# Four z blocks and five gate blocks named ahead of the query stage, an order edge behind them, and a fifth query and key buffer

## The chip, the core and the metric

The kernel runs on one core of one Trainium2 chip. The metric is the device time of one execution in microseconds; lower is better. A measured value is the median of several runs, and one execution is profiled.

## What is computed

One layer of a hybrid encoder over 1024 tokens of width 1024, all in float32. A shared RMS norm and one wide input projection feed two branches: a Hyena branch (two gated long convolutions) and an attention branch with low-rank queries and keys. The lines that matter here:

```
h = rms_norm(x, g_norm);  proj = h @ w_in
hy_in, z_hy, c_q, c_kv, k_rope, z_attn, gate_hy, gate_attn = split(proj)
... hyena branch: zc from hy_in by two long convolutions, u_hy = (zc * silu(z_hy)) @ w_hy_out
q  = rms_norm(c_q, g_cq) @ w_uq            # 8 heads of 96
kv = rms_norm(c_kv, g_ckv) @ w_ukv         # 64 key columns and 64 value columns a head
q, k = rms_norm per head, rotary on the last 32 columns (the key's come from k_rope)
u_attn = (softmax(q k^T) v * silu(z_attn)) @ w_attn_out
gates = sigmoid([gate_hy, gate_attn] + b_gate)
out = x + (g_hy * u_hy + g_at * u_attn) @ w_out
```

## The kernel before, in words

**Tiling.** Everything is done in blocks of 128 rows or columns. A float32 operand of a product is split into a high and a low part (`split`, L138 on ScalarE and L139 on VectorE; `gsplit`, L142 and L143, the same with a scale), and each product is three matmuls: high by high, low by high, high by low (`mm3`, L119 to L122).

**Projection blocks.** `proj_block` (L567) makes one block of 128 columns of `proj` for all tokens: 48 matmuls of 128x512, in two halves of 24. Each half loads a weight tile `wr` on the SP queue (L559, two buffers) and splits it into `wh` and `wl` (four buffers each). The result lies in two PSUM banks `pm` out of four, so that two blocks can be under way. Three kinds of blocks matter: `fill_c` (query and key latents, `cT`), `fill_z` (four blocks of `z_attn`; a sigmoid on ScalarE at L673, then VectorE, then a store on SP) and `fill_g` (sixteen gate blocks; a sigmoid at L683 and a store that ScalarE issues, L684). Their sigmoids free the banks.

**The stages.** After the norm and the filter spectra, with gate blocks 0 to 7 among them, come the convolutions (`convs`), then `qkv`, then `attention`, then the output products. `qkv` makes queries, keys and values for eight tiles of 128 tokens, in four pairs (`hf` 0 to 3). Its weights pass through `wst` (two buffers: three loads of `w_uq` at L735, then two of `w_ukv`; then the rotary table `rt` at L753 and the raw rotary key `kr` at L764 use the same buffers). Per tile: six query products in `pq` (two banks, 18 matmuls of 128x384, evicted by L795 into `q`), products of keys and values in `pkv` (12 matmuls of 128x512, evicted by L799 and L800 into `k` and `v`). The rotary key is transposed for all tiles at once (`pkr`, L767), and every tile's key norm needs it. Per pair: sums of squares (L803 to L808), a reciprocal root on VectorE (`rsqrt`, L152 to L158), the scaling of the queries (L813), their rotary part (`rot`, L827 to L830), the keys on GpSimd (L818, L819), and stores of `q` and `k` on SP (L822). `q` and `k` have four buffers each, and a buffer is free when its store has landed.

**What comes behind.** `load_pair` (L838) loads the first two heads' queries, keys and values back (`qr`, `kr`, `vr`). `attention` opens PSUM pools in the banks that the projection blocks held, so it starts behind the last block's sigmoid. It begins with transposes (L862) into `pth`, split by L142 into `qh`, `kh`. The weights of the Hyena output (`branch_out`, L981, `wr` with two buffers; split by ScalarE at L138 and by GpSimd at L139) are loaded early too.

**What sets the order.** No order is written by hand. A scheduler at build time gives every engine its instruction list: of what it holds to be ready by its own cost estimates, it takes first what stands earlier in the program. So instructions that stand later can be placed in the gaps of earlier ones. On the chip each engine then runs its list in order. A call of `behind` (used by `mm3` for its first matmul) adds an edge: that instruction is not placed before another one. In the program, `qkv` stands ahead of the four z blocks and of gate blocks 8 to 15.

Of the kernel before, what the change touches and what calls it, by code (L numbers as in the profile page):

```python
# [10 lines left out]
F32 = mybir.dt.float32  # L11
# [8 lines left out]
P = 128  # L20
# [3 lines left out]
H = 8  # L24
# [9 lines left out]
GEARLY = 8  # L34
# [59 lines left out]
class K:  # L94
# [457 lines left out]
    def proj_block(self, c0, m=P):  # L552

        nc, wp = self.nc, self.wp
        ps = [self.pp.tile([P, 512], F32, tag="mm", bufs=MMB, name=self.nm("pm")) for _ in range(2)]
        src = self.a["w_in"][0].rearrange("(d p) c -> p d c", p=P)
        for g in range(2):
            raw = wp.tile([P, 4, P], F32, tag="wr", bufs=2, name=self.nm("wr"))
            nc.sync.dma_start(out=raw[:, :, 0:m], in_=src[:, 4 * g:4 * g + 4, c0:c0 + m])  # L559
            wh = wp.tile([P, 4, P], F32R, tag="wh", bufs=4, name=self.nm("wh"))  # L560
            wl = wp.tile([P, 4, P], F32R, tag="wl", bufs=4, name=self.nm("wl"))
            self.split(raw[:, :, 0:m], wh[:, :, 0:m], wl[:, :, 0:m])
            for i in range(4):
                d = 4 * g + i
                for (w, h, f) in ((wh, self.hh, 0), (wh, self.hl, 1), (wl, self.hh, 2)):
                    for c in range(2):
                        nc.tensor.matmul(ps[c][0:m], lhsT=w[:, i, 0:m], rhs=h[d][:, c * 512:(c + 1) * 512],  # L567
                                         start=(d == 0 and f == 0), stop=(d == 7 and f == 2))
        return ps

# [150 lines left out]
    def qkv(self, kp):  # L721

        nc, a = self.nc, self.a
# [4 lines left out]
        wqh = kp.tile([P, 3, 768], F32R, tag="wqh", name="wqh")  # L728
        wql = kp.tile([P, 3, 768], F32R, tag="wql", name="wql")
        wkh = kp.tile([P, 2, 1024], F32R, tag="wkh", name="wkh")  # L730
        wkl = kp.tile([P, 2, 1024], F32R, tag="wkl", name="wkl")
        def weights(nme, n, w, wh, wl):
            for c in range(n):
                r = kp.tile([P, w], F32, tag="wst", bufs=2, name=self.nm("wst"))
                nc.sync.dma_start(out=r, in_=a[nme][0, c * P:(c + 1) * P])  # L735
                self.split(r, wh[:, c], wl[:, c])

        def latent(hf, i):
# [4 lines left out]
            self.gsplit(r, self.gcq[:, i:i + 1] if i < 3 else self.gckv[:, i - 3:i - 2], h_, l_)  # L743
            return h_, l_

        weights("w_uq", 3, 768, wqh, wql)
        C = {(0, i): latent(0, i) for i in range(3)}
        weights("w_ukv", 2, 1024, wkh, wkl)
# [29 lines left out]
        for hf in range(4):  # L778
# [5 lines left out]
            for j in range(2):  # L784
                tt = 2 * hf + j
                ts = slice(j * P, (j + 1) * P)
                q = kp.tile([P, H, 96], F32, tag="q", bufs=4, name=self.nm("q"))
                k = kp.tile([P, H, 96], F32, tag="k", bufs=4, name=self.nm("k"))
                v = kp.tile([P, H, 64], F32, tag="v", bufs=2, name=self.nm("v"))
                for g in range(2):  # L790
                    hs = slice(4 * g, 4 * g + 4)
                    ps = self.pp.tile([P, 4, 96], F32, tag="cv", bufs=CVB, name=self.nm("pq"))
                    for c in range(3):
                        self.mm3(ps, ch[c][:, ts], cl[c][:, ts], wqh[:, c, g * 384:(g + 1) * 384], wql[:, c, g * 384:(g + 1) * 384], c == 0, c == 2)
                    nc.scalar.activation(out=q[:, hs], in_=ps, func=AF.Copy, scale=rq0[:, tt:tt + 1])  # L795
                    ps = self.pp.tile([P, 4, 2, 64], F32, tag="tp", bufs=2, name=self.nm("pkv"))
                    for c in range(2):
                        self.mm3(ps, ch[3 + c][:, ts], cl[3 + c][:, ts], wkh[:, c, g * 512:(g + 1) * 512], wkl[:, c, g * 512:(g + 1) * 512], c == 0, c == 1)
                    nc.scalar.activation(out=k[:, hs, 0:64], in_=ps[:, :, 0], func=AF.Copy, scale=rk0[:, tt:tt + 1])  # L799
                    nc.scalar.activation(out=v[:, hs], in_=ps[:, :, 1], func=AF.Copy, scale=rk0[:, tt:tt + 1])  # L800
                nc.sync.dma_start(out=self.vd[:, :, tt].rearrange("b p j c -> p b (j c)"), in_=v.rearrange("p (b j) c -> p b (j c)", j=2))
                sq = kp.tile([P, H, 96], F32, tag="sqq", bufs=2, name=self.nm("sqq"))
                nc.scalar.activation(out=sq, in_=q, func=AF.Square)  # L803
                nc.vector.tensor_reduce(out=ssq[:, j, 0], in_=sq, axis=AX.X, op=ALU.add)
                sk = kp.tile([P, H, 64], F32, tag="sqq", bufs=2, name=self.nm("sqk"))
                nc.scalar.activation(out=sk, in_=k[:, :, 0:64], func=AF.Square)
                nc.vector.tensor_reduce(out=ssq[:, j, 1], in_=sk, axis=AX.X, op=ALU.add)
                nc.vector.tensor_scalar(out=ssq[:, j, 1], in0=ssq[:, j, 1], scalar1=ssr[:, tt:tt + 1], scalar2=None, op0=ALU.add)  # L808
                QK.append((tt, q, k))
# [384 lines left out]
def hyena_mla_kernel(ctx, tc, a, out):  # L1194
# [4 lines left out]
    with k.pool("pp", space=PSUM) as k.pp:  # L1199
        with ExitStack() as sr:  # L1200
# [33 lines left out]
            k.rp = srp.enter_context(k.pool("rp"))  # L1234
            k.raw = {}
            k.load_pair(0)
            for b in range(4):
                k.fill_z(b)
            for b in range(GEARLY, 16):
                k.fill_g(b)  # L1240
            k.hyena_tiles(yp)
    with k.pool("gp2", side="right") as g2:
# [50 lines left out]
```

## Time and profile before

| what | us |
|---|---|
| median of 3 runs (1146.56 to 1151.04) | 1148.81 |
| the profiled execution's own time | 1145.55 |
| its span | 1143.8 |
| TensorE busy in the span | 1094.3 (96%) |
| VectorE busy | 893.9 (78%) |
| ScalarE busy | 588.0 (51%) |
| GpSimd busy | 108.3 (9%) |

The mean granted TensorE clock is 0.997 of full speed. The profiled execution is 3.26 us (0.28%) shorter than the median of the runs, and 1.75 us of its time lie outside the span. Engines in the profile: PE is TensorE's matmuls, PEld its weight loads, DVE is VectorE, ACT is ScalarE, POOL is GpSimd, SP is the engine that issues most loads; SPq is its queue. A busy PE says nothing of how well it is used, and shares over the whole span mix stages; the stage between the convolutions and the attention runs from about 618 to 719 us.

### The profile page before, as it was taken

The page shows a single profiled execution, that of the slowest core. Times are in us where ns is not written, and L with a number is a line of the kernel's source. Part 1 is how long each engine was busy: PE and PEld are TensorE (multiplying, and loading weights), DVE is VectorE, ACT ScalarE, POOL GpSimd, SP SyncE. Part 2 cuts the span into 40 slices and gives each one's busy share as a digit, 9 for nine tenths or more (in the row PEclk, how much of TensorE's full clock was granted, in tenths as well). Part 3 has the DMA queues.
Part 4 walks back from the last instruction along what each step waited for, and adds up shares of the span by engine and source line. Part 5 has one row for each costly group of instructions (what it writes and reads, how often), then busy time and mean ns, then how long its engine had stood idle before and what let it go on. Part 6 is the DMA issues. An engine that isn't in the chain of part 4 may idle for free.

```text
span 1143.8 us, 15469 instructions
## 1 busy us (share of the span) xinstructions
PE 1094.3 (96%) x5525; PEld 905.2 (79%) x5525; DVE 893.9 (78%) x1583; ACT 588.0 (51%) x1101; POOL 108.3 (9%) x112
## 2 busy tenths in 40 slices
PE   4899999999999999999999989899999999999998
PEld 3678888888888888878887878687887878777886
DVE  6988798688788985768865795688788888468984
ACT  6745645754435534533433752787877777221420
POOL 0000000000000000000000042202200000114345
PEclk9989999999999999999999999999999999999999
DMA  5446455642234325234236557501302000897064
GB/s 213 134 147 195 154 166 181 202 123 67 88 92 129 112 85 163 84 95 130 84 92 202 154 157 248 184 29 50 117 5 98 1 19 11 268 312 269 29 198 165
DMA packets 119221, 150.27 MB, mean 131 GB/s; under 512 B 8548, under 2 KB 82408, under 8 KB 119144
## 3 DMA queue, kind: packets, MB, share of 16 engines
q1 hardware_dynamic: 107400, 120.45, 34.2%
q10 hardware_dynamic: 11744, 28.84, 6.7%
q8 instruction: 43, 0.70, 0.3%
q14 instruction: 34, 0.28, 0.1%
HBM read 101.81 MB, written 47.45 MB: 131 GB/s over the span
## 4 chain that ended last, share of the span: by engine, by line
PE 71%; DVE 13%; ACT 6%; DMA 5%; issue 2%; POOL 0%; SPq 0%; ACTq 0%; DVEq 0%; POOLq 0%
PE pm L567 31%; PE pu L128 8%; PE pt L907 4%; PE pi L128 4%; PE pmo L121 2%; PE pmo L119 2%; PE pmo L122 2%; PE S L119 2%; PE S L122 2%; ACT pr L893 2%; PE S L121 2%; PE pv L919 2%; PE pv L920 2%; PE po L119 1%; PE po L122 1%
## 5 line engine op out<-in xcount | busy, mean ns | idle before, releaser
L567 PE MATMUL pm<-hh,wh 128*128 128x512 f32 x656 | 208.8, 394 | 1.8 <-DVE hl L143 0.9
L567 PE MATMUL pm<-hl,wh 128*128 128x512 f32 x656 | 209.0, 394 | 0.0
L567 PE MATMUL pm<-hh,wl 128*128 128x512 f32 x656 | 208.5, 393 | 0.1
L138 ACT CAST wh<-wr 128x512 fp32r<-128x512 f32 x98 | 60.2, 621 | 169.2 <-PE pm L567 107.4
L567 PEld LDWEIGHTS pm<-hh,wh 128*128 128x128 f32 x656 | 123.2, 189 | 27.6 <-DVE hl L143 1.1
L567 PEld LDWEIGHTS pm<-hh,wl 128*128 128x128 f32 x656 | 123.3, 188 | 25.8 <-DVE wl L139 0.5
L567 PEld LDWEIGHTS pm<-hl,wh 128*128 128x128 f32 x656 | 123.0, 188 | 25.2
L138 ACT CAST PTh<-pt 128x512 fp32r<-128x512 f32 x128 | 72.8, 587 | 40.8 <-PE pt L907 39.3
L139 DVE TENSOR_TENSOR PTl<-pt,PTh 128x512 fp32r<-128x512 f32 x128 | 83.8, 682 | 10.6 <-ACT PTh L138 10.1
L891 DVE TENSOR_REDUCE mx<-S 128x1 f32<-128x1024 f32 x64 | 77.9, 1217 | 11.5 <-PE S L122 11.3
L907 PE MATMUL pt<-ident,pr 128*128 128x128 f32 x512 | 75.3, 276 | 3.6 <-ACT pr L893 1.4
L139 DVE TENSOR_TENSOR wl<-wr,wh 128x512 fp32r<-128x512 f32 x95 | 66.1, 700 | 15.5 <-ACT wh L138 15.3
L893 ACT ACTIVATE pr<-S,mx 128x1024 f32<-128x1024 f32 x64 | 71.7, 1120 | 5.2 <-DVE mx L891 4.9
L907 PEld LDWEIGHTS pt<-ident,pr 128*128 128x128 f32 x512 | 58.5, 140 | 19.4 <-DVE PTl L139 5.1
L919 PE MATMUL pv<-PTh,vc 128*128 128x256 f32 x256 | 69.1, 298 | 0.4 <-DVE at L930 0.4
L920 PE MATMUL pv<-PTl,vc 128*128 128x256 f32 x256 | 67.9, 293 | 0.0
L473 DVE TENSOR_TENSOR t<-pu,kt 128x512 f32<-128x512 f32 x64 | 41.1, 682 | 31.6 <-PE pu L128 31.0
L138 ACT CAST rh<-res 128x512 fp32r<-128x512 f32 x64 | 39.5, 619 | 41.7 <-PE pu L128 19.9
L119 PE MATMUL S<-kh,qh 96*128 96x512 f32 x128 | 53.0, 414 | 2.6 <-ACT pr L893 2.4
L121 PE MATMUL S<-kh,ql 96*128 96x512 f32 x128 | 52.2, 408 | 0.0
L919 PEld LDWEIGHTS pv<-PTh,vc 128*128 128x128 f32 x256 | 48.5, 190 | 4.6 <-DVE at L930 1.9
L122 PE MATMUL S<-kl,qh 96*128 96x512 f32 x128 | 51.5, 403 | 0.0
(285 smaller groups left out, 2385.5 us busy)
## 6 DMA issues: line engine op xcount, KB each, us to landing
wr<-in_w_in_dram SPq DMA_DIRECT2D x82, 256.0 KB, 3.2
wor<-in_w_out_dram SPq DMA_DIRECT2D x36, 256.0 KB, 4.3
dec<-in_dec_dram SPq DMA_DIRECT2D x16, 512.0 KB, 3.7
gT<-ob ACTq DMA_DIRECT2D x16, 512.0 KB, 3.0
gg<-gT SPq DMA_DIRECT2D x16, 512.0 KB, 4.7
kd<-kt ACTq DMA_DIRECT2D x28, 256.0 KB, 2.1
kt<-kd SPq DMA_DIRECT2D x28, 256.0 KB, 2.7
m<-gg ACTq DMA_DIRECT2D x16, 256.0 KB, 5.1
```

The source lines that it names most:

```text
L119: m = nc.tensor.matmul(out, lhsT=lh, rhs=rh, start=start, stop=False)
L121: nc.tensor.matmul(out, lhsT=ll, rhs=rh, start=False, stop=False)
L122: nc.tensor.matmul(out, lhsT=lh, rhs=rl, start=False, stop=stop)
L128: m = self.nc.tensor.matmul(out, lhsT=x, rhs=y, start=n == 0, stop=n == len(ops) - 1)
L138: self.behind(self.nc.scalar.copy(out=hi, in_=x), after)
L139: (eng or self.nc.vector).tensor_tensor(out=lo, in0=x, in1=hi.bitcast(F32), op=ALU.subtract)
L567: nc.tensor.matmul(ps[c][0:m], lhsT=w[:, i, 0:m], rhs=h[d][:, c * 512:(c + 1) * 512], start=(d == 0 and f == 0), stop=(d == 7 and f == 2))
L891: nc.vector.tensor_reduce(out=mx, in_=ps, axis=AX.X, op=ALU.max, negate=True)
L893: i = nc.scalar.activation(out=pr, in_=ps, func=AF.Exp, bias=mx, accum_out=RS[h // 2][:, qb, h % 2:h % 2 + 1])
L907: nc.tensor.transpose(out=pt[:, i], in_=pr[:, kb * P:(kb + 1) * P], identity=self.ident)
L919: nc.tensor.matmul(pv, lhsT=V[h][:, kb], rhs=hi[:, kb], start=(kb == 0), stop=False)
L920: nc.tensor.matmul(pv, lhsT=V[h][:, kb], rhs=lo[:, kb], start=False, stop=(kb == 7))
```

## The change

The four z blocks and gate blocks 8 to 12 are written inside `qkv`, ahead of its weight loads; gate blocks 13 to 15 stay where they were. The last matmul of block 12 is kept in `lastmm`, and the first query matmul (tile 0, first half of the heads, first slice) gets an edge behind it. The `q` and `k` tiles get five buffers in place of four, which takes 2 x 3072 bytes more in each partition. Arithmetic, loads and stores are the same in number and size.

```diff
@@ proj_block
-                        nc.tensor.matmul(ps[c][0:m], lhsT=w[:, i, 0:m], rhs=h[d][:, c * 512:(c + 1) * 512],
+                        self.lastmm = nc.tensor.matmul(ps[c][0:m], lhsT=w[:, i, 0:m], rhs=h[d][:, c * 512:(c + 1) * 512],
@@ qkv
+        for b in range(4):
+            self.fill_z(b)
+        for b in range(GEARLY, 13):
+            self.fill_g(b)
+        first = self.lastmm
         weights("w_uq", 3, 768, wqh, wql)
@@ qkv, for each tile
-                q = kp.tile([P, H, 96], F32, tag="q", bufs=4, name=self.nm("q"))
-                k = kp.tile([P, H, 96], F32, tag="k", bufs=4, name=self.nm("k"))
+                q = kp.tile([P, H, 96], F32, tag="q", bufs=5, name=self.nm("q"))
+                k = kp.tile([P, H, 96], F32, tag="k", bufs=5, name=self.nm("k"))
...
-                        self.mm3(ps, ch[c][:, ts], cl[c][:, ts], wqh[:, c, g * 384:(g + 1) * 384], wql[:, c, g * 384:(g + 1) * 384], c == 0, c == 2)
+                        self.mm3(ps, ch[c][:, ts], cl[c][:, ts], wqh[:, c, g * 384:(g + 1) * 384], wql[:, c, g * 384:(g + 1) * 384], c == 0, c == 2,
+                                 first if tt == 0 and g == 0 and c == 0 else None)
@@ hyena_mla_kernel
-            for b in range(4):
-                k.fill_z(b)
-            for b in range(GEARLY, 16):
+            for b in range(13, 16):
                 k.fill_g(b)
```

## Rows read from the trace of the kernel before

**Rows 1.** Chain that ended last, 600 to 745 us: start us, us, what.

```profile
618.19 5.74 DMA wst<-in_w_uq_dram
...
637.84 4.37 DMA kr<-cT
...
655.88 2.67 DVE q L813 x2
...
693.56 2.68 DVE q L813 x2
...
700.71 3.98 DMA qd<-q
...
706.16 6.78 DMA wr<-in_w_hy_out_dram
...
716.23 3.97 DMA wr<-in_w_hy_out_dram
```

**Rows 2.** Three stretches: length, then busy us (count) of PE, PEld, DVE, ACT, POOL.

```profile
622.70:642.20 19.50, 16.21 (x81) 13.72 (x79) 13.43 (x22) 13.93 (x26) 0.00 (x0) 1.00 0.88 280
...
655.90:683.50 27.60, 24.66 (x122) 21.47 (x122) 26.74 (x60) 17.37 (x37) 11.92 (x10) 1.00 0.51 153
...
683.50:700.70 17.20, 17.20 (x77) 14.21 (x77) 16.68 (x39) 5.71 (x11) 7.48 (x7) 1.00 0.69 216
```

**Rows 3.** Timeline of PE: start us, us, line, tile; idle before it and releaser in brackets.

```profile
625.25 0.62 PE L119 MATMUL pq<-wqh,ch 128*128 128x384 f32 x2 [2.18 <-ACT ch L142]
...
633.66 0.44 PE L119 MATMUL pq<-wqh,ch 128*128 128x384 f32 x1
...
642.26 0.71 PE L767 MATMUL pkr<-ident,kr 64*128 64x64 f32 x8 [0.98 <-DMA kr<-cT]
...
666.59 0.45 PE L119 MATMUL pq<-wqh,ch 128*128 128x384 f32 x1 [2.03 <-ACT q L795]
...
683.57 0.63 PE L567 MATMUL pm<-hh,wh 128*128 128x512 f32 x2
...
717.14 0.61 PE L567 MATMUL pm<-hh,wl 128*128 128x512 f32 x2
...
719.31 1.08 PE L862 MATMUL pth<-ident,qr 128*96 128x128 f32 x8 [1.55 <-ACT ob L683]
```

**Rows 4.** Timeline of ACT, columns as in the timeline of PE.

```profile
517.07 1.08 ACT L673 ACTIVATE ob<-pm 128x512 f32<-128x512 f32 x2
...
617.97 1.26 ACT L683 ACTIVATE ob<-pm,cols 128x512 f32<-128x512 f32 x2
...
661.77 0.47 ACT L799 ACTIVATE k<-pkv,ry 128x256 f32<-128x256 f32 x1 [2.63 <-DMA kdr<-k]
...
665.95 1.05 ACT L795 ACTIVATE q<-pq,ry 128x384 f32<-128x384 f32 x2 [2.62 <-DMA qd<-q]
...
696.11 1.26 ACT L683 ACTIVATE ob<-pm,cols 128x512 f32<-128x512 f32 x2
...
712.96 1.37 ACT L138 CAST wh<-wr 128x512 fp32r<-128x512 f32 x2 [15.59 <-DMA wr<-in_w_hy_out_dram]
...
714.24 1.26 ACT L683 ACTIVATE ob<-pm,cols 128x512 f32<-128x512 f32 x2
...
718.05 0.62 ACT L138 CAST wh<-wr 128x512 fp32r<-128x512 f32 x1 [2.55 <-DMA wr<-in_w_hy_out_dram]
...
718.58 1.26 ACT L683 ACTIVATE ob<-pm,cols 128x512 f32<-128x512 f32 x2
```

**Rows 5.** PE groups by shape, first 622.6 to 642 us, then 683.5 to 718.5 us.

```profile
L119 PE MATMUL pq<-wqh,ch 128*128 128x384 f32 x20 | 7.0, 356 | 2.3 <-ACT ch L142 2.2
...
L567 PE MATMUL pm<-hh,wh 128*128 128x512 f32 x50 | 15.4, 390 | 0.0
```

**Rows 6.** Timeline of DVE around the last pair, columns as before.

```profile
691.38 0.68 DVE L139 TENSOR_TENSOR wl<-wr,wh 128x512 fp32r<-128x512 f32 x1
```

**Rows 7.** DMA issues from 600 to 725 us: KB each, median us to landing.

```profile
qr<-qd SPq DMA_DIRECT2D x1, 768.0 KB, 4.2
```

## The prediction, made before the change was run

> **What bounds the kernel now.** The change touches the stage between the convolutions and the attention, about 618 to 719 us, so I read that stage alone. First comes the chain of waits [rows 1]: what is to be seen is that from 618 us on it hardly runs over matmuls. It goes from a load of w_uq (618.19) over that of the raw rotary key (lands 642.2) to VectorE, which does the norms and rotations of the four pairs one behind the other (the scaling of the first pair's queries at 655.88, of the last pair's at 693.56), then over the last store of queries (700.71) to two loads of the Hyena output's weights, the second ending at 720.2. The busy times by stretch say the same [rows 2]: from 655.9 to 683.5 VectorE is busy 26.74 of 27.60 us (97%) and TensorE 24.66 (89%); from 683.5 to 700.7 VectorE 16.68 of 17.20. TensorE's timeline [rows 3] shows where it stands still: 2.18 us for the first query product, 0.98 for the rotary key's transposes, 2.03 for a free bank, 1.55 ahead of the attention. ScalarE's timeline [rows 4] shows why the attention starts at 719.31 and not earlier: the sigmoid of gate block 14 runs at 714.24 and that of block 15 at 718.58, each behind a cast of Hyena weights that ScalarE has ahead of it in its list and for which it waits 15.59 us (until 712.96) and 2.55 us (until 718.05). Block 15's last matmuls begin at 717.14 and end at 717.75, so there the two ends are only 0.8 us apart; of TensorE's own idle time little would be needed to part them.
>
> **The change part by part.** Sums are made on the profiled execution (1145.55 us, span 1143.8); the median of the runs, 1148.81, lies 3.26 above it.
>
> *The nine blocks.* The sigmoids of the z blocks run from 517.07 on, and that of gate block 11 at 617.97 [rows 4], ahead of the first query product at 625.25 [rows 3]. So eight of the nine blocks, with their weight loads on SP, their z stores on SP and their gate stores from ScalarE, are early already, and naming them earlier removes and adds nothing there; GpSimd's list has none of them. What really moves is the second half of block 12. From 683.57 on there are 150 matmuls `pm`, three groups of 50 [rows 3, 5], where three blocks have 144: six of block 12 are left for the end, and 18 were strewn among tile 0's query products. At (717.75 - 683.57) / 150 = 0.228 us a matmul the 24 take 5.5 us.
>
> *The edge.* All 24 now stand ahead of the first query product. The first half ends near 623.1 (625.25 less 2.18 of idle time), so they end at 628.5, and the 2.18 us are covered, since what that product waited for was there by 625.2. But the stage does not get ahead by it. By 642.2 TensorE had done 18 matmuls of block 12 and 60 query products (three groups of 20 [rows 5]) and then waited 0.98 us for the rotary key, whose load comes out of the `wst` buffers: that is a chain of loads, casts and subtractions that begins at 618.19 [rows 1] and asks nothing of the query products. A query product takes (641.28 - 633.66) / 42 = 0.18 us, where 641.28 is 642.26 less its wait and 42 the products past the first tile [rows 3]. From 628.5 on, 54 to 60 of them end at 638.2 to 639.3, and TensorE waits three to four us for the same load. The idle time moves from one place to the other; up to the rotary key the gain is 0, and so is the loss while fewer than (642.2 - 628.5) / 0.18 = 76 products stand ahead of it. Behind the edge wait 144 query products and all that follows in TensorE's list; ScalarE's evictions of tile 0 wait with them, but in the trace those came near 633, and 628.5 plus 18 products is 631.7. I take 0; the ends are 3.3 us of gain, all of TensorE's idle time from 622.7 to 642.2 (19.50 - 16.21 [rows 2]), and the loss of the fourth rival.
>
> *The tail.* With block 12 done before, 144 matmuls remain behind the query stage: TensorE is through 6 x 0.228 = 1.4 us earlier. That is on the path only if the sigmoids are; I take 0, and 1.4 as the end.
>
> *Five buffers.* Tile 4 then writes its queries and keys without waiting for tile 0's stores: ScalarE's waits of 2.63 and 2.62 us [rows 4] go, and with them TensorE's 2.03, and 2.94 of idle time in that stretch at most [rows 2]. What is late next is VectorE, which was not idle then. It can gain what it stood still, 27.60 - 26.74 + 17.20 - 16.68 = 1.4 us, and one subtraction of gate weights of 0.68 us [rows 6], since block 12's weight buffers come free before the stage and not at 683 us, so that one of three such pieces can leave the last 17 us. I take half of the first and the second: 0.7 + 0.7 = 1.4 us earlier at the last store, and so at the Hyena weights, at ScalarE and at the attention's start. Ends: 0 and 2.1. The 6 KB more in each partition shift later buffers; in the rows of the first loads behind the stage I see no wait that hangs on it, and cost it at 0. Were a load to wait for a later store instead, it would be for the last one, which it follows anyway.
>
> On those 2.94 us: ScalarE waits for two stores just when TensorE stands still 2.03 us [rows 3, 4]. [...]
>
> Sum: 0 + 0 - 1.4 = -1.4 us. 1145.55 becomes 1144.2, the median 1148.81 becomes **1147.4**. Behind 719 us and ahead of 618 us I take the order as it was.
>
> **The rivals.**
>
> *TensorE decides after all.* If the scheduler puts the sigmoids of blocks 14 and 15 ahead of the Hyena casts, the attention starts when TensorE is through. At most it gets back 3.3 + 2.9 = 6.2 us [rows 2]: blocks through at 711.6, attention at 713.1, time 1142.6. The loaded queries allow it: the load of `qr` takes 4.2 us [rows 7] behind the store that lands at 704.7 [rows 1], so about 709. For it speaks that the two ends are only 0.8 us apart; against it that ScalarE's list put both casts first and that the first 3.3 us move to another wait. Chance 0.24.
>
> *Nothing happens.* The nine blocks were early, the gaps close in one place and open in another, and VectorE goes on as it did: 1148.8. Chance 0.19.
>
> *ScalarE's wait slides a block forward (slower).* If the scheduler puts the Hyena cast ahead of block 13's sigmoid, that sigmoid goes from 696.11 to 714.24 [rows 4]. Block 15 needs block 13's two banks, so its 48 matmuls (48 x 0.228 = 10.9 us) start behind it, end near 725.2 in place of 717.75, and the attention starts 7.4 us later: 1156.2. It decides as soon as that cast is listed one block (10.9 us) earlier than now. Block 13 itself moves by only 1.4 us, so I give it 0.07.
>
> *Five tiles ahead of the rotary key.* With five buffers 90 query products fit ahead of its transposes: 628.5 + 90 x 0.18 = 644.7, 2.5 us past the load, and VectorE's chain is late by that: 1151.3. From 76 products on it counts. Only 60 stood there with room for 72, so 0.08.
>
> **How the numbers follow.** The forecast, a gain of 0.5 to 4 us, has 0.42. The range reaches from 1141.0 (the first rival with the 1.4 us of the tail or the 1.55 us at the attention's start on top) to 1152.0 (the fourth rival with the runs' scatter); it leaves out the slower rival and little else. About 0.5% (5.7 us) is what a measurement of this kernel can tell from no change, so faster means below 1143.1 and slower above 1154.5. Three quarters of the first rival's chance lie below: faster 0.18. Slower is the third rival: 0.07. The rest is 0.75.
>
> **What would show it.** In the profile after: first query product near 628.5 without a wait, a longer wait ahead of the rotary key's transposes near 642, no waits of ScalarE for stores at tile 4, VectorE still near 97% busy from 656 to 700, 144 `pm` matmuls at the end, and ScalarE's wait for the Hyena weights still ahead of the last sigmoids. The attention's first transpose should stand at 716 to 719. I am wrong if the rotary key lands much earlier or later than 642, if the last sigmoids run directly behind their matmuls, or if the order ahead of 618 us or inside the attention has changed by more than the stage.

## The result and the profile after

The kernel after takes 1153.99 us (median of 11 runs, 1152.27 to 1157.06), the kernel before 1147.8 us (median of 11, 1144.89 to 1153.79). The ratio is 1.0055 [1.0042, 1.0069]: slower by 0.55%, where I had forecast 1147.4 us and no change that can be told. The profiled execution of after took 1153.56 us with a span of 1151.8, 8.0 us more than both were before; the medians are 6.2 apart, since the profiled execution of before lies 2.25 below its median and that of after 0.43. The mean granted clock is 0.989 (before 0.997). No engine got more to do; TensorE's 5 us more (1099.4, before 1094.3) are products at a lower clock, as will be seen:

The page of the kernel after, busy time of each engine:

```profile
PE 1099.4 (95%) x5525; PEld 910.2 (79%) x5525; DVE 895.5 (78%) x1583; ACT 588.9 (51%) x1101; POOL 109.4 (9%) x112
```

**TensorE.** Its timeline in the kernel after (start us, us, line, tile; in brackets the idle time before it and what ended it), beside [rows 3]:

```profile
629.22 0.34 PE L119 MATMUL pq<-wqh,ch 128*128 128x384 f32 x1
...
637.89 0.45 PE L119 MATMUL pq<-wqh,ch 128*128 128x384 f32 x1 [1.93 <-ACT q L801]
...
644.04 0.71 PE L772 MATMUL pkr<-ident,kr 64*128 64x64 f32 x8 [1.88 <-DMA kr<-cT]
...
718.84 0.61 PE L567 MATMUL pm<-hh,wl 128*128 128x512 f32 x2
725.12 1.94 PE L868 MATMUL pth<-ident,qr 128*96 128x128 f32 x8 [5.66 <-ACT ob L683]
```

The first query product comes at 629.22 without a wait, as the edge wants it. Then there are waits that before did not have: 1.93 us for a query bank, 1.88 for the rotary key (0.98 in [rows 3]), and 5.66 us ahead of the attention, where 1.55 stood. The last projection product ends at 719.45, 1.7 us later than before, but the attention starts 5.8 us later.

**ScalarE.** Its timeline in the kernel after, beside [rows 4]; first the stretch behind block 12, then the last two gate sigmoids with the Hyena casts:

```profile
632.11 1.05 ACT L138 CAST wkh<-wst 128x1024 fp32r<-128x1024 f32 x1 [1.91 <-DMA wst<-in_w_ukv_dram]
...
633.88 1.25 ACT L683 ACTIVATE ob<-pm,cols 128x512 f32<-128x512 f32 x2
...
635.52 1.05 ACT L138 CAST wkh<-wst 128x1024 fp32r<-128x1024 f32 x1
...
637.28 1.03 ACT L801 ACTIVATE q<-pq,ry 128x384 f32<-128x384 f32 x2
641.42 0.62 ACT L138 CAST wh<-wr 128x512 fp32r<-128x512 f32 x1 [3.11 <-DMA wr<-in_w_in_dram]
641.95 0.84 ACT L809 ACTIVATE sqq<-q 128x768 f32<-128x768 f32 x1
...
708.39 1.27 ACT L683 ACTIVATE ob<-pm,cols 128x512 f32<-128x512 f32 x2 [9.32 <-PE pm L567]
...
719.19 1.35 ACT L138 CAST wh<-wr 128x512 fp32r<-128x512 f32 x2 [9.53 <-DMA wr<-in_w_hy_out_dram]
723.86 0.62 ACT L138 CAST wh<-wr 128x512 fp32r<-128x512 f32 x1 [3.33 <-DMA wr<-in_w_hy_out_dram]
724.38 1.26 ACT L683 ACTIVATE ob<-pm,cols 128x512 f32<-128x512 f32 x2
```

The first cast, the evictions and tile 0's squares before, from ScalarE's timeline in the kernel before:

```profile
630.48 1.05 ACT L138 CAST wkh<-wst 128x1024 fp32r<-128x1024 f32 x1 [1.27 <-DMA wst<-in_w_ukv_dram]
...
633.05 1.03 ACT L795 ACTIVATE q<-pq,ry 128x384 f32<-128x384 f32 x2
634.11 0.85 ACT L803 ACTIVATE sqq<-q 128x768 f32<-128x768 f32 x1
```

Three places matter. Block 12 is now finished before tile 0, and ScalarE's list has its sigmoid and the second cast of key weights ahead of tile 0's query evictions: from the first cast to the evictions it takes 5.17 us instead of 2.57. Those evictions run at 637.28, though the products were done by 633.3. Behind them stands the cast of block 13's second weight half, which waits 3.11 us for its load; tile 0's squares (`sqq`) come behind it, at 641.95 instead of 634.11. And at the end the sigmoid of block 15, whose products are done at 719.45, stands behind three Hyena casts, the last of which waits for its load until 723.86.

**VectorE and the clock.** Busy times by stretch in the kernel after (length, then busy us and count of PE, PEld, DVE, ACT, POOL, granted clock, DMA share, GB/s):

```profile
618.65:656.55 37.90, 33.72 (x149) 28.52 (x148) 22.12 (x53) 23.32 (x47) 0.00 (x0) 0.91 0.69 208
658.90:706.70 47.80, 46.76 (x226) 40.82 (x225) 45.98 (x101) 24.94 (x52) 19.49 (x16) 1.00 0.52 159
...
725.10:735.00 9.90, 8.82 (x28) 6.26 (x28) 4.53 (x6) 6.74 (x10) 4.06 (x5) 0.55 0.74 242
...
637.90:642.20 4.30, 4.26 (x14) 3.94 (x14) 2.74 (x6) 1.19 (x3) 0.00 (x0) 0.60 1.04 284
...
644.00:648.60 4.60, 4.56 (x18) 3.69 (x19) 2.50 (x8) 1.21 (x3) 0.00 (x0) 0.63 0.31 87
```

The stretches of the kernel before that answer to the first three:

```profile
618.00:655.90 37.90, 34.55 (x169) 29.16 (x168) 25.18 (x68) 26.58 (x56) 0.00 (x0) 1.00 0.68 205
655.90:700.70 44.80, 41.86 (x198) 35.69 (x198) 43.42 (x98) 23.08 (x47) 19.41 (x16) 1.00 0.58 177
719.30:731.00 11.70, 8.91 (x48) 6.19 (x48) 6.64 (x9) 8.72 (x14) 4.07 (x5) 1.00 0.84 279
```

In the first 37.9 us of the stage VectorE does 22.12 us of work instead of 25.18. What it could not begin then (tile 0's norms need the late evictions and squares) it does behind: 45.98 us of work in the 47.8 us from the first scaling of queries to its last rotation, where before 43.42 lay in 44.8. It is 96 to 97% busy in both, so the 3 us come out as time. And TensorE is granted 0.60 and 0.63 of its full clock right behind its two waits near 640, and 0.55 behind the 5.66 us ahead of the attention; in the profiled execution of the kernel before, the stretches that answer to these ran at 1.00 (above).

The chain of waits of the kernel after (start us, us, what), beside [rows 1]:

```profile
658.88 2.67 DVE q L819 x2
...
699.61 2.68 DVE q L819 x2
...
706.75 3.03 DMA qd<-q
...
712.11 7.79 DMA wr<-in_w_hy_out_dram
...
721.18 2.66 DMA wr<-in_w_hy_out_dram
...
724.38 0.69 ACT ob L683
```

From the first pair on it is the chain of before with later times: +3.0 at the first pair, +6.0 at the last pair, at the store and at the first load of Hyena weights. The casts that wait for these loads run 6.2 and 5.8 us later than in [rows 4]. Ahead of the first pair the chain runs over the rotary key (1.8 us later) and the products of keys and values behind it, and these stand in the stretch at 0.63 of the clock: eleven of them start between 644.68 and 648.66, where the same eleven lie 2.38 us apart in the kernel before (642.90 to 645.28, clock 1.00), so the clock takes about 1.6 us here (an estimate from these rows). **Where the 8 us lie:** block 11's sigmoid, ahead of all this, is 0.63 us later (618.60, before 617.97 [rows 4]); from there to the attention's start 5.18 more are lost (106.52 us, before 101.34); from the attention's start to the last of its 64 row maxima 2.28 (246.91, before 244.63), of which 1.52 lie ahead of the first row maximum, in the stretch at the halved clock. Sum 8.09; the last row maximum is 8.09 us later, the whole span 8.0.

### The profile page after: what moved, and what is told of

Its sections match the earlier page's. It is cut to its first block, busy times and chain, and to the rows that moved or that the text cites. A ratio compares the mean times of both kernels' runs of the same rounds, so it can differ in the third digit from the quotient of the medians.

```text
span 1151.8 us, 15463 instructions
## 1 busy us (share of the span) xinstructions
PE 1099.4 (95%) x5525; PEld 910.2 (79%) x5525; DVE 895.5 (78%) x1583; ACT 588.9 (51%) x1101; POOL 109.4 (9%) x112
## 4 chain that ended last, share of the span: by engine, by line
PE 64%; DVE 14%; DMA 10%; ACT 6%; issue 4%; POOL 1%; SPq 0%; POOLq 0%; ACTq 0%; DVEq 0%
PE pm L567 33%; PE pu L128 8%; PE pt L913 4%; PE pi L128 4%; DMA wor<-in_w_out_dram 3%; PE S L119 2%; PE S L122 2%; PE S L121 2%; ACT pr L899 2%; PE pv L925 2%; PE pv L926 2%; DMA m<-gg 1%; PE pth L868 1%; DVE mo L139 1%; ACT PTh L138 1%
```

## The experiments

Times from one run to another are compared from block 11's sigmoid on, since that stands ahead of all edits. "Chain end" below means the start of VectorE's last rotation less that sigmoid: 82.4 us before, 87.85 after. The engines' lists as built say what the edit does: without the edge the kernel after has the same list on every engine, so the edge orders nothing that would not stand so anyway; with only z blocks and gate blocks 8 to 11 moved, four buffers and no edge, the lists are those of the kernel before. Block 12 alone is what moves.

### The two halves of the change, and the rotary key

Five buffers on the kernel before, and the move without them:

```diff
before_five_bufs (on before)
-                q = kp.tile([P, H, 96], F32, tag="q", bufs=4, name=self.nm("q"))
-                k = kp.tile([P, H, 96], F32, tag="k", bufs=4, name=self.nm("k"))
+                q = kp.tile([P, H, 96], F32, tag="q", bufs=5, name=self.nm("q"))
+                k = kp.tile([P, H, 96], F32, tag="k", bufs=5, name=self.nm("k"))
moved_four_bufs (on after)
-                q = kp.tile([P, H, 96], F32, tag="q", bufs=5, name=self.nm("q"))
-                k = kp.tile([P, H, 96], F32, tag="k", bufs=5, name=self.nm("k"))
+                q = kp.tile([P, H, 96], F32, tag="q", bufs=4, name=self.nm("q"))
+                k = kp.tile([P, H, 96], F32, tag="k", bufs=4, name=self.nm("k"))
...
-                                 first if tt == 0 and g == 0 and c == 0 else None)
+                                 None)
```

> The kernel before with five query and key buffers and nothing else. Theory A (the place of block 12 makes the loss, the buffers do not): ScalarE's two waits for stores at tile 4 (2.63 and 2.62 us) are gone, VectorE goes on as it did, ratio to before 0.997 to 1.001. Theory B (the buffers make the loss, by the 6 KB that they shift or by what TensorE then does first): ratio 1.003 to 1.007.

> The nine blocks moved, without the edge and with four buffers. Theory A: the loss stays, the attention's start is 5 to 8 us later than before, and the waits for stores at tile 4 may come on top: ratio 1.004 to 1.008. Theory B: ratio 0.998 to 1.001.

**Measured:** five buffers alone 1.0024 [1.0009, 1.0039], the move alone 1.0066 [1.0041, 1.0090]. With the move the chain ends at 88.8 us without and at 87.85 with five buffers: they are worth about 1 us there (1.4 forecast), and the loss is the move's, as theory A has it. But five buffers alone are no gain either: 1.0024 lies between the two theories, and the two ratios do not add up to the 1.0055 of the whole change. Timeline of PE in before_five_bufs:

```profile
713.45 0.61 PE L567 MATMUL pm<-hh,wl 128*128 128x512 f32 x2
719.99 1.94 PE L862 MATMUL pth<-ident,qr 128*96 128x128 f32 x8 [5.93 <-ACT ob L683]
```

Busy times by stretch in before_five_bufs, columns as above:

```profile
660.00:700.00 40.00, 40.00 (x191) 34.70 (x190) 38.72 (x93) 18.91 (x38) 15.57 (x14) 1.00 0.62 189
...
719.00:725.00 6.00, 4.31 (x17) 3.24 (x18) 1.97 (x3) 4.98 (x9) 3.86 (x5) 0.50 0.79 226
725.00:731.00 6.00, 4.80 (x21) 3.54 (x20) 3.47 (x4) 3.84 (x6) 0.74 (x1) 0.83 0.73 265
```

TensorE has no idle time left from 660 to 700 and is through with the blocks 3.7 us earlier than before [rows 3], but the attention waits for the same sigmoid as before. The scattered idle time becomes one gap of 5.93 us, and behind it the clock is 0.50. From the attention's start to the last row maximum it takes 245.93 us instead of 244.63. ScalarE's two waits for stores are down to 0.90 and 0.83 us.

The next suspect was the rotary key: 32 query products stand ahead of its transposes in TensorE's list and trace (the expectations below say 29), 60 before. This run puts them behind tile 2's last query product:

```diff
after_rotary_later (on after)
-            nc.tensor.transpose(out=pkr[:, tt], ...
+            kts.append(nc.tensor.transpose(out=pkr[:, tt], ...
...
+                    if tt == 2 and g == 1:
+                        self.behind(kts[0], qm)
```

> The kernel after, with the rotary key's transposes kept behind the last query product of tile 2, so that about 50 query products stand ahead of them in place of 29. Theory A in its narrow form (too few query products ahead of the rotary key, so that VectorE gets the sums of squares of tiles 2 and 3 too late): the last pair's scaling comes at 694 to 697 us in place of 699.6, ratio 0.999 to 1.003. Theory C (the products cannot run ahead since ScalarE empties their banks late, whatever the list of TensorE says): the transposes then come later than 644 and the last pair at 699 to 702, ratio 1.005 to 1.008.

**Measured:** 1.0047 [1.0030, 1.0064]. The transposes run at 648.58 instead of 644.04, with no wait, and the last pair's queries are scaled at 699.98 (after: 699.61). So 54 products ahead of the rotary key in place of 32 bring nothing while tile 0's evictions are late (636.81 here) and the rotary key comes 4.5 us later, as theory C has it; which of the two takes the gain away, this run does not part.

### ScalarE's Hyena casts

The second suspect is the wait in front of block 15's sigmoid. The kernel before already sets some orders by hand (`hyena_split`, L1007, behind a softmax); these casts it leaves to the scheduler. First the casts go behind that sigmoid, then behind the last split of the first head's keys:

```diff
after_late_casts (on after)
-            nc.scalar.activation(out=ob[:, sl], ...
+            self.lastsig = nc.scalar.activation(out=ob[:, sl], ...
...
-            self.split(r, wh, wl, nc.gpsimd if self.mb == 1 else nc.vector)
+            self.split(r, wh, wl, nc.gpsimd if self.mb == 1 else nc.vector, self.lastsig if self.mb == 1 else None)
after_casts_behind_keys (on after); before_casts_behind_keys, five_bufs_casts_behind_keys (the same on the other two)
-            self.gsplit(ps[0:96], ...
+            i = self.gsplit(ps[0:96], ...
+            if h == 0 and j == 3:
+                self.firstkey = i
...
-            self.split(r, wh, wl, nc.gpsimd if self.mb == 1 else nc.vector)
+            self.split(r, wh, wl, nc.gpsimd if self.mb == 1 else nc.vector, self.firstkey if self.mb == 1 else None)
```

> The kernel after, with the casts of the first Hyena output weights kept behind the last gate sigmoid on ScalarE. If ScalarE's wait for those weights sets the start of the attention: last sigmoid directly behind its matmuls near 719.5 us in place of 724.4, TensorE not idle for 5.7 us and at full clock from there on (the 2.2 us lost at half clock come back): 5 to 7 us less than after, ratio 0.999 to 1.001. If the chain over the last store of queries sets it by itself (the loads of queries and keys): the attention starts at 723 to 725 as now and the ratio stays 1.004 to 1.006.

> The kernel after, with the three casts of Hyena output weights kept behind the splits of the first head's keys on ScalarE, so that neither the last gate sigmoid nor the first head's queries wait for them. If ScalarE's wait for those weights is what holds the attention back: first transposes near 720.5, first row maximum near 726.5 in place of 732.6, full clock, ratio to before 1.000 to 1.003. If the loads of queries and keys behind VectorE's late chain hold it back anyway: first maximum at 730 or later, ratio 1.0035 to 1.006.

**Measured:** after_late_casts 1.0035 [1.0016, 1.0054]. Its timeline of ACT and of PE:

```profile
719.72 1.26 ACT L683 ACTIVATE ob<-pm,cols 128x512 f32<-128x512 f32 x2 [9.61 <-PE pm L567]
...
725.45 0.62 ACT L138 CAST wh<-wr 128x512 fp32r<-128x512 f32 x1 [3.44 <-DMA wr<-in_w_hy_out_dram]
725.97 1.25 ACT L142 ACTIVATE qh<-pth,gq 96x512 fp32r<-96x512 f32 x2
```

```profile
720.46 1.08 PE L868 MATMUL pth<-ident,qr 128*96 128x128 f32 x8 [0.55 <-ACT ob L683]
727.49 1.94 PE L868 MATMUL pth<-ident,kr 128*96 128x128 f32 x8 [5.95 <-DVE ql L143]
```

The sigmoid is free and the attention starts at 720.46, but the third cast is now next in ScalarE's list, ahead of the first query split. The wait has only moved, and TensorE's gap with it (5.95 us); the ratio lies between the two forecasts. With all casts behind the keys (1.0020 [1.0000, 1.0040], in the first forecast) the attention starts 101.15 us behind the marker, as early as before (101.34), though the chain still ends at 87.6. What is left lies behind that start: 247.05 us to the last row maximum, with the clock at 0.74 from 719 to 725 and at 0.69 from 725 to 731 (scores at 0.43 us a step from 723.11 to 726.52), though no wait of TensorE is longer than 1.44 us there.

### The late evictions

```diff
after_first_eviction_early (on after)
+            if b == 12 and c == 0:
+                self.sig12 = i
...
+                    if tt == 0 and g == 1:
+                        self.behind(self.sig12, i)
```

> The kernel after with block 12's first sigmoid kept behind tile 0's query evictions on ScalarE, which also lets 38 query products and 6 matmuls of block 13 stand ahead of the rotary key in place of 29 and 12. If ScalarE's late eviction of tile 0 is what makes VectorE late: last rotation at most 85.5 us behind gate block 11's sigmoid (before 82.4, after 87.9), ratio 1.001 to 1.004. If block 12's second half ahead of the first product makes it whatever ScalarE does: 87 us or more, ratio 1.0045 to 1.0065.

**Measured:** 1.0018 [1.0001, 1.0034]. The chain ends at 82.55 us, where it stood before (82.4); both are as the first forecast has it. The timeline of ACT in this run:

```profile
634.08 0.56 ACT L803 ACTIVATE q<-pq,ry 128x384 f32<-128x384 f32 x1
...
636.43 0.56 ACT L803 ACTIVATE q<-pq,ry 128x384 f32<-128x384 f32 x1
636.90 0.68 ACT L683 ACTIVATE ob<-pm,cols 128x512 f32<-128x512 f32 x1
```

Tile 0's first half is evicted at 634.08, by the marker 3.0 us earlier than in the kernel after. VectorE's work in the first 36.6 us of the stage is 25.15 us again. So 5.3 of the 5.45 us that the chain lost come back with this order on ScalarE. The edge changes more than tile 0's evictions, though: the cast of block 13's weights now stands behind tile 0's squares, which run at 637.47 instead of 641.95; on TensorE 38 query products and 6 matmuls of block 13 stand ahead of the rotary key instead of 32 and 12; and the clock stays at 1.00 from 635 to 642. The attention starts 101.49 us behind the marker, as before. What is left of the loss lies behind that start: TensorE was idle for 4.09 us ahead of it, waiting for the sigmoid behind the Hyena casts, the clock is 0.50 from 725 to 731, and it takes 247.25 us to the last row maximum.

A second way to take work out of that stretch is to keep block 13's products, 12 of which slipped in between tile 0 and tile 1, behind the last product of keys and values:

```diff
after_block13_behind (on after)
-                k.fill_g(b)
+                k.fill_g(b, k.lastpkv)
```

> The kernel after with gate block 13 kept behind the last product of keys and values, so that none of its matmuls stands among the first query products. If ScalarE holds the second tile's products back, TensorE only waits longer: last rotation 87 to 88.5 us behind gate block 11's sigmoid, block 15 ends 2.7 us later, ratio 1.005 to 1.0075. If those 12 matmuls take the place of query products: last rotation at 84 to 86 us, ratio 1.001 to 1.004.

**Measured:** 1.0064 [1.0041, 1.0086]. The chain ends at 85.7 us, 2 us better than after, and the time is no better: the chain is that of the second forecast, the time that of the first. Tile 0's evictions and squares are as late here as in the kernel after (637.56 and 642.53); the products of keys and values behind the rotary key run at the full clock from 644 to 649. So about 2 of the 5.45 us hang on what lies between tiles 0 and 1 on TensorE, with the clock behind it, and these 2 and the 5.3 above overlap. Timeline of ACT in this run:

```profile
716.90 0.62 ACT L138 CAST wh<-wr 128x512 fp32r<-128x512 f32 x1 [16.80 <-DMA wr<-in_w_hy_out_dram]
717.43 1.26 ACT L685 ACTIVATE ob<-pm,cols 128x512 f32<-128x512 f32 x2
...
722.75 0.62 ACT L138 CAST wh<-wr 128x512 fp32r<-128x512 f32 x1 [3.55 <-DMA wr<-in_w_hy_out_dram]
723.27 1.26 ACT L685 ACTIVATE ob<-pm,cols 128x512 f32<-128x512 f32 x2
```

A Hyena cast now stands ahead of block 14's sigmoid and waits 16.80 us, so that it runs at 717.43 (708.39 in the kernel after): the kind of mishap that my slower rival described, one block later.

### Both causes at once, and the casts without the move

> The kernel before with the three Hyena casts kept behind the first head's key splits and nothing else. TensorE is through only 0.8 us ahead of the last sigmoid here, so the start of the attention gains 0.5 to 1.0 us and no more: ratio 0.998 to 1.0005. If the later casts collide with the first steps of the attention: ratio 1.0005 to 1.003.

> The kernel before with five buffers and the same three casts moved back. With five buffers TensorE is through its last gate block near 714 and then stands idle; if only ScalarE's casts keep it so, first transposes near 715.3 and first row maximum near 721.5 (before: 725.3), ratio 0.994 to 0.998, faster than both kernels. If the loads of keys and values, which the Hyena weights follow, hold the start: first maximum at 724 or later, ratio 0.998 to 1.001.

The edit of after_eviction_and_casts is that of after_first_eviction_early and of after_casts_behind_keys together.

> The kernel after with both edges, block 12's first sigmoid behind tile 0's evictions and the Hyena casts behind the first keys. If the two losses are separate and add: ratio 0.998 to 1.001, against 1.0055 for the kernel after and 1.002 with the casts alone. If a late VectorE costs nothing once the casts are out of the way: 1.001 to 1.003, as with the casts alone.

**Measured:** the kernel before with late casts 1.0009 [0.9991, 1.0027]; with five buffers as well 0.9983 [0.9967, 0.9999]; the kernel after with both edges 0.9991 [0.9978, 1.0005]. With both waits treated the change's loss is gone. The two are not separate losses that add, though. Either edge alone brings the attention's start back to where it was before (101.49 and 101.15 us, before 101.34), for late loads cost the start only while it waits for the casts; with both it comes at 97.51, 3.8 us earlier than before. That gain is taken back behind the start (249.94 us to the last row maximum), where a split waits for the third cast and the first product of probabilities and values (733.04) 3.13 us for that split. The casts alone are worth nothing to the kernel before, where the attention has no earlier start to gain: its products end only 0.8 us ahead of the sigmoid. In that run the start comes at 101.46 us, the clock is 0.91 from 700 to 740, with scores at 0.43 us a step from 724.87 to 728.28 behind waits of 0.55 and 1.43 us, and it takes 247.22 us to the last row maximum. But with five buffers the attention starts at 713.77, 5 us earlier by the marker, and the time falls by 2 us: the start is ahead of the first forecast (715.3), the ratio in the second. Timeline of PE in five_bufs_casts_behind_keys, and of ACT:

```profile
713.77 1.08 PE L862 MATMUL pth<-ident,qr 128*96 128x128 f32 x8 [0.55 <-ACT ob L683]
...
729.41 0.55 PE L921 MATMUL pv<-PTh,vc 128*128 128x256 f32 x1 [2.12 <-ACT PTh L138]
```

```profile
728.17 0.62 ACT L138 CAST wh<-wr 128x512 fp32r<-128x512 f32 x1 [3.57 <-DMA wr<-in_w_hy_out_dram]
```

The third cast waits again, now inside the attention, ahead of a split of probabilities. Two last runs move it and the later ones behind the seventh softmax:

```diff
five_bufs_casts_behind_softmax; after_eviction_casts_softmax (on five_bufs_casts_behind_keys; on after_eviction_and_casts)
+            if u == 5:
+                self.soft6 = last
...
-            self.split(r, wh, wl, ..., self.firstkey if self.mb == 1 else None)
+            self.split(r, wh, wl, ..., (self.firstkey if d < 2 else self.soft6) if self.mb == 1 else None)
```

> Edit on the kernel before: five query and key buffers, the first two Hyena casts of ScalarE behind the first head's last key split, and the third and later ones behind the seventh softmax. With all three behind the key split the attention started 5.5 us earlier than in the kernel before (713.77 against 719.31) but the row maxima of the first head's eleventh block only 1 us earlier, because the third cast waited 3.57 us for its load at 728.17 and held up the split of the first probabilities, so that the first product of probabilities and values waited 2.12 us. Theory: ScalarE's in-order wait is what takes the gain back; without it that product waits under 0.6 us, and the gain stays at 3 to 5 us up to the end: ratio 0.9955 to 0.9975. Rival: something else takes it back (GpSimd's splits of the values, or the granted clock): ratio 0.998 to 1.000, with the wait still there or replaced by one on GpSimd.

> Edit on the kernel after: tile 0's query evictions ahead of block 12's sigmoid, the first two Hyena casts behind the first key split, the third and later ones behind the seventh softmax. With all three behind the key split it was 0.9991 of the kernel before, with a wait of 3.13 us ahead of the first product of probabilities and values. Theory: that wait goes, and the kernel comes to 0.996 to 0.998 of the kernel before, so that the change as such costs nothing once both waits of ScalarE are out of its way. Rival: moving block 12 costs something of its own behind the stage: ratio 0.9985 to 1.001.

**Measured:** 0.9963 [0.9944, 0.9981] and 0.9974 [0.9963, 0.9985]. Both lie in their first forecast and beat both kernels; the first, without the moved blocks, has the lowest ratio of this study, but its interval overlaps that of the second. But for one of 3545.2 us, the executions of the first spread from 1139.57 to 1148.04 us, and the profiled one is the shortest, so what is read from its trace is more than what the ratio says. The same casts without a fifth buffer and without the move were not run. Timeline of ACT in five_bufs_casts_behind_softmax:

```profile
741.69 0.62 ACT L138 CAST wh<-wr 128x512 fp32r<-128x512 f32 x1
```

The cast runs without a wait, no wait of TensorE over 1.5 us is left from 714 to 760, and the gain stays: the attention starts 5.1 us earlier than before by the marker and its last row maximum stands 4.6 us earlier. In after_eviction_casts_softmax the start is 3.0 us earlier, and the last row maximum 0.8: the clock is 0.72 there from 719 to 725 (scores at 0.43 us a step from 721.57 to 724.12), again with no wait longer than 1.45 us.

### The clock by itself

Is it the gap that halves the clock? Twenty-four products that nobody reads, ahead of block 15's own, fill it:

```diff
five_bufs_thrown_away (on before_five_bufs), after_thrown_away (on after)
-    def proj_block(self, c0, m=P):
+    def proj_block(self, c0, m=P, extra=0):
...
+            for x in range(extra if g == 0 else 0):
+                nc.tensor.matmul(ps[x % 2], lhsT=wh[:, 0], rhs=self.hh[0][:, 0:512], start=True, stop=True)
...
-        ps = self.proj_block(3232 + b * P, P)
+        ps = self.proj_block(3232 + b * P, P, 24 if b == 15 else 0)
```

These runs do more work than the reference asks for.

> The kernel before with five buffers, and 24 matmuls ahead of gate block 15 whose results are overwritten: they keep TensorE busy until the attention starts near 720, all else as in the run with five buffers alone (1.0024). If the idle stretch and the half clock behind it make that loss: full clock from 720 on, second row maximum near 728 in place of 732.9, ratio 0.998 to 1.0005, although more work is done. If the buffers themselves make it (what they shift in memory or in the lists): ratio 1.0015 to 1.004 as without them.

> The kernel after with the same 24 matmuls ahead of gate block 15: TensorE is busy until about 724.9, the attention starts at 725.6. If the half clock behind TensorE's wait of 5.7 us costs 2.2 us: second row maximum near 732.5 in place of 734.7, ratio 1.0025 to 1.0045 in place of 1.0055. If it costs nothing, the 24 matmuls cost 0 to 0.6 us: ratio 1.005 to 1.007.

**Measured:** 1.0006 [0.9991, 1.0021] with five buffers (1.0024 without the thrown products; the two intervals overlap, so it is the stretches below that carry the reading), 1.0050 [1.0033, 1.0067] on the kernel after: just above the first forecast the one, at the start of the second the other. Busy times by stretch in five_bufs_thrown_away:

```profile
719.00:725.00 6.00, 4.32 (x23) 2.90 (x24) 2.81 (x5) 5.33 (x8) 4.02 (x5) 1.00 0.76 228
725.00:731.00 6.00, 4.83 (x28) 3.53 (x27) 4.09 (x5) 3.57 (x7) 0.00 (x0) 1.00 0.89 300
```

and in after_thrown_away:

```profile
725.00:731.00 6.00, 4.30 (x21) 2.86 (x20) 2.81 (x4) 5.14 (x8) 3.62 (x5) 0.88 0.67 223
731.00:737.00 6.00, 6.00 (x20) 4.61 (x19) 2.45 (x2) 2.69 (x5) 0.00 (x0) 0.55 0.92 336
```

In the first the gap is 0.58 us, the clock stays at 1.00, and the stretch from the attention's start to the last row maximum takes 244.72 us, as before. In the second the gap is gone too (0.55 us), the transposes run at the full clock, but it falls five us later, in the middle of the first scores, to 0.55 of the full one, and the stretch takes 246.84 us. Why it falls there and not in the other run, whose idle times in that place are alike, these runs do not settle.

Nor does one execution say what the clock costs. The 109 executions of the kernel before that were timed beside these experiments have mean granted clocks from 0.988 to 0.997; the 16 at 0.997 took 1145.1 us on average, the 8 at 0.989 took 1150.2. So the clock falls in the kernel before too, in some executions, and the profiled one (0.997) is one of the least disturbed. The kernel after lies at 0.986 to 0.991 in all its eleven, before_five_bufs at 0.987 to 0.993 (median 0.991), and with the gap filled (five_bufs_thrown_away) at 0.989 to 0.997 (median 0.9945) in ten of its twelve executions, the other two having taken 1225.84 and 6216.68 us. That the clock is higher with the gap filled is thus seen in more than the profiled pair; that the low clock costs 1.3 or 2.3 us is not.

## Why the prediction was wrong

**The nine blocks: right.** Eight of the nine were early already, and only block 12's second half moves.

**The edge: the step that failed.** It is a step of that paragraph, not the edge as such, which orders nothing. I said that up to the rotary key "the gain is 0, and so is the loss". The half of it that I looked at was right: the first query product stands at 629.22 (forecast 628.5), without a wait, and the idle time moved to the rotary key's transposes, which stand at 644.04 by their load. The half that failed is the sentence on ScalarE: that tile 0's evictions, "near 633" in the trace, would follow the products' end at 631.7. They came at 637.28. I had counted what waits behind the edge on TensorE, and of block 12 only its matmuls. But its sigmoid is an instruction of ScalarE: with block 12 complete it was listed ahead of tile 0's evictions, and the second cast of key weights too. Behind them came the cast of block 13's weights, with its 3.11 us of wait ahead of tile 0's squares. After_first_eviction_early sets tile 0's evictions and squares ahead again, and the chain ends at 82.55 instead of 87.85 us. So the term that I set to 0 measured 5.45 us in the chain, of which this order on ScalarE gives back 5.3. How much of it is the late evictions, the cast, block 13's matmuls or the clock behind TensorE's waits is not parted: after_block13_behind gives back 2.2 with the evictions as late as ever. The forecast of 54 to 60 query products ahead of the rotary key (32 came) fell with it; after_rotary_later, with 54 of them, ends its chain no earlier. The rotary key I had at 642.2 as before; it came at 644.04, 1.2 us later by the marker. The fourth rival, more than 76 products ahead of it, did not come.

**VectorE as the bound: right, and not used.** I took VectorE at 97% as the reason why more buffers bring little. The same row says that what delays its first work in the stage can hardly be made up later: it did 3.1 us less up to the first pair, and its chain ended 5.45 us later.

**Five buffers: size right, value wrong.** The waits of tile 4 went and the chain ended 0.8 to 1 us earlier, against 1.4 forecast. In the time this is lost: 1.0024 on the kernel before. TensorE's gaps from 660 to 700 were for want of a buffer, since the fifth closed them altogether (40.00 busy of 40 us, before 37.06); but VectorE, busy for 38.62 of these 40 us before, did hardly more with five (38.72), and the kernel got no faster until ScalarE's casts were moved as well, when both together gave 0.37%.

**The tail: later, and not free.** TensorE is through 1.7 us later instead of 1.4 earlier, and the attention starts at 725.12, where I forecast 716 to 719. TensorE's idle time I costed at nothing. Where it collected in one place it may have had a price: behind the gap of 5.66 us in the kernel after and that of 5.93 with five buffers, the stretch from the attention's start to the last row maximum took 2.3 and 1.3 us more than before in the profiled executions.

**The rivals.** "TensorE decides after all" needed the casts behind the sigmoids; the scheduler did not do that, but once it was made to, the time fell by 0.26% with the moved blocks (after_eviction_casts_softmax) and by 0.37% without them, 3.0 and 4.2 us of the 6.2 that I gave it. The slower rival named the right instructions, ScalarE's in-order wait for Hyena casts, yet not how it came to cost: no cast slid ahead of block 13's sigmoid; the casts stayed ahead of block 15's, and what they wait for came about 6 us later. I gave slower 0.07 because I asked only whether the order of that wait would change, not whether what it waits for would be late.

## What to carry to other kernels

When a block of work is moved ahead, list what it makes ready on every engine, not only on the one that it occupies: an in-order engine that serves two streams can have the moved block's instructions first, and the other stream pays (here ScalarE: tile 0's evictions at 637.28 in place of 633.05). Where an engine is busy for all the rest of a stage (here VectorE, 96 to 97%), what delays its first instruction is the cost to look for: its last one came 5.45 us later here. The delay reaches the next stage only where something waits for it: here either edge alone gave the attention its old start back (101.49 and 101.15 us, before 101.34). And look for in-order waits on far-off loads (here casts for the next stage) that stand ahead of an instruction which frees a bank: they bind two stages together, and taking them away was worth more here than the change, with five buffers and once all three places where the wait can land were cleared.

## What was not expected of the hardware

TensorE's granted clock falls to near half in stretches behind some idle time: in the kernel after to 0.60 and 0.63 behind waits of 1.93 and 1.88 us near 640 and to 0.55 behind the gap of 5.66 us, with scores at 0.43 us a step instead of 0.23, and with five buffers alone to 0.50 behind the gap of 5.93 us. By what rule it falls, these runs do not show. The length of a wait alone does not tell: those of 2.18 and 2.03 us in the kernel before [rows 3] had no such effect (1.00 from 618 to 700.7), and the clock fell behind waits of at most 1.47 us in after_thrown_away (0.55 from 731 to 737), before_casts_behind_keys (0.91 from 700 to 740), after_casts_behind_keys (0.74 from 719 to 725) and after_eviction_casts_softmax (0.72 from 719 to 725). Nor is it the same in every execution of one kernel: 0.988 to 0.997 in that before. So a price of 1 to 2.5 us (an estimate from the 1.3 and 2.3 us above) belongs to an idle stretch only as a possible one, to be read from the granted clock behind it, in more than one execution.
